# Two-layer trunk: the feed-forward's first tiles kept in PSUM, the last x tile taken last, and 128-column matmuls behind 512-column ones

## The chip, the core and the metric

The kernel runs on one core of a Trainium2 chip. The metric is the device time of one execution in microseconds; the time before is the median of three runs. Engines are named as in the profile: PE (TensorE, matrix multiplies), PEld (its loads of weights), DVE (VectorE), ACT (ScalarE), POOL (GpSimd) and SP (SyncE, which issues most transfers). PSUM, where PE writes its sums, has eight banks of 128 x 512 float32: four in a pool "acc", four in a pool "aux".

## What is computed

A trunk of two layers over 512 positions of width 1024. Each layer is a mixer (gated linear attention and sparse attention in the first, retention in the second) and a feed-forward; the change touches the feed-forward alone, which runs twice, with D_FF = 2816, or 22 tiles of 128.

```python
def rmsnorm(x, g):
    return x * rsqrt(mean(x * x, axis=-1) + EPS) * g

def swiglu(h, w_gate, w_up, w_down):
    return (silu(h @ w_gate) * (h @ w_up)) @ w_down

for layer in range(2):
    h = h + mixer(rmsnorm(h, attn_norm[layer]), ...)
    h = h + swiglu(rmsnorm(h, ffn_norm[layer]), w_gate[layer], w_up[layer], w_down[layer])
return rmsnorm(h, final_norm)
```

## The kernel before

x is held transposed: eight tiles X[0] to X[7] of 128 features x 512 positions. Every float32 product is done in three matmuls of a rounded type. A matrix is split in a high part (ACT rounds it: wh for weights, xh for x) and what is left (DVE subtracts: wl, xl), and `mm3` issues high x high, low x high and high x low. A weight slab is 128 x 1024; `slab()` hands out the next one of a fixed list and prepares two ahead of it: a transfer by SP, wh by ACT and wl by DVE (L176, L178). Three wh and three wl buffers go round, so the wh of a slab waits until PE has done with the slab three before it or one that came free sooner.

`ffn` (L722 and after) has these stages:

- The first two f tiles, f=0 and f=1, by plain projections: gate and up, each 24 matmuls of 512 columns (8 tiles of x, three matmuls each; `proj_b`), 96 in all. The norm's factor rb is applied behind the matmul: g = gate x rb, u = up x rb (L806, L807), then `act`: silu on ACT, the product on DVE, and the split of the result into ah and al.
- Between the projections, `mixed(k)` for k = 0 to 3 makes sums and differences of the halves (in positions and in features) of x: tn, split into ch and cl, and td, split into dh and dl. DVE and ACT take turns at it.
- The other 20 f tiles in ten rounds i = 0 to 9 of seven products, P1, P2, P7, P6, P5, P3 and Q4: a scheme that makes a 2 x 2 block product in seven block products where the plain way takes eight. Each product is 24 matmuls of 256 columns. P7 and P6 read ch and cl, Q4 reads dh and dl, P1, P5, P2 and P3 read halves of xh and xl; `n1()` makes the half that P5 and the later P1 need. P1, P6, P5 and P3 of a round add up in one PSUM bank, q["z"]; behind P1, P6 and P5 ACT copies the running sum out (c, L830 and L838) before the next product adds to it. P7 and Q4 add up in another bank, P2 has a bank of its own.
- From round 2 on, down-projections "D" of tiles that are done stand between the products: 18 matmuls of 512 columns each, into aux, added to X. The list EVENTS sets the order of products and D; `after` makes for each product a generator with its work on DVE and ACT, and `follow()` takes one step of each at every event.

Each engine runs its own instructions in a fixed order, which a scheduler sets when the kernel is built, by its estimates of when things will be ready; at run time an instruction that waits holds up all behind it on its engine. So the order of the code is a wish: the order of instructions on an engine is shown below where the text needs it.

Of the kernel before, what the change touches and what calls it, by code (L numbers as in the profile page):

```python
# [16 lines left out]
P = 128  # L17
# [30 lines left out]
def trunk(ctx: ExitStack, tc: tile.TileContext, a, out):  # L48
# [17 lines left out]
    def tt_(name, dt=F32, n=512):  # L66
        return tp.tile([P, n], dt, tag="t", name=name)
# [117 lines left out]
    def slab():  # L185
        while len(ready) <= AHEAD and state["i"] < len(sched):
            prepare()
        return ready.pop(0)

    def mm3(ps, ops, start=True, stop=True, skip=False):  # L190
        n = len(ops)
        for i, (lh, ll, rh, rl) in enumerate(ops):
            nc.tensor.matmul(ps, lh, rh, start=start and i == 0, stop=False, skip_group_check=skip)  # L193
            nc.tensor.matmul(ps, lh, rl, start=False, stop=False, skip_group_check=skip)  # L194
            nc.tensor.matmul(ps, ll, rh, start=False, stop=stop and i == n - 1, skip_group_check=skip)  # L195

# [90 lines left out]
    def new_rb():  # L287
        return cp.tile([P, T], F32, tag="rb", name="rb")
# [8 lines left out]
    def proj_b():  # L297
        wh, wl = slab()
        ps = acc()
        mm3(ps, [(wh[:, k * P:(k + 1) * P], wl[:, k * P:(k + 1) * P], XH[k], XL[k]) for k in range(KT)])  # L300
        return ps
# [418 lines left out]
    def ffn(box, g0, final, halves=False):  # L720
# [10 lines left out]
        def gain(k):  # L731
            return sm[:, g0 + k:g0 + k + 1]

        def mixed(k):

            x12, tn, td = tt_("x12"), tt_("tn"), tt_("td")
            nc.scalar.activation(x12[:, lo], X[k][:, hi], AF.Copy, scale=gain(k))
            nc.vector.scalar_tensor_tensor(tn[:, lo], X[k + 4][:, hi], gain(k + 4), x12[:, lo],
                                           op0=ALU.mult, op1=ALU.subtract)
            nc.scalar.activation(CH_[k][:, lo], tn[:, lo], AF.Copy)  # L740
            nc.vector.scalar_tensor_tensor(tn[:, hi], X[k][:, lo], gain(k), tn[:, lo], op0=ALU.mult, op1=ALU.add)
            nc.scalar.activation(CH_[k][:, hi], tn[:, hi], AF.Copy, scale=-1.0)
            nc.vector.scalar_tensor_tensor(td[:, lo], X[k + 4][:, lo], gain(k + 4), tn[:, hi],
                                           op0=ALU.mult, op1=ALU.subtract)
            d = HALF[k % 2]
            nc.scalar.activation(DH_[k // 2][:, d], td[:, lo], AF.Copy, scale=-1.0)
            nc.vector.tensor_sub(CL_[k][:, lo], tn[:, lo], CH_[k][:, lo].bitcast(F32))
            nc.vector.scalar_tensor_tensor(CL_[k][:, hi], tn[:, hi], -1.0, CH_[k][:, hi].bitcast(F32),
                                           op0=ALU.mult, op1=ALU.subtract)
            nc.vector.scalar_tensor_tensor(DL_[k // 2][:, d], td[:, lo], -1.0, DH_[k // 2][:, d].bitcast(F32),  # L750
                                           op0=ALU.mult, op1=ALU.subtract)

# [19 lines left out]
            "Q4": [(DH_[k // 2][:, HALF[k % 2]], DL_[k // 2][:, HALF[k % 2]]) for k in range(4)],  # L772
        }

        def product(ps, w, name, start):

            for gu in range(2):
                cols = [slice(gu * 512 + k * P, gu * 512 + (k + 1) * P) for k in range(4)]
                mm3(ps[:, HALF[gu]], [(w[0][:, cols[k]], w[1][:, cols[k]]) + forms[name][k] for k in range(4)],
                    start=start and gu == 0, skip=True)  # L780

        def act(f, g, u, neg):

# [11 lines left out]
            AH[f] = (ah, al)  # L795


        rb = None
        for f in range(2):
            pg = proj_b()  # L800
            if rb is None:
                rb = norm_b(box["acc"], D, new_rb())
            mixed(2 * f)
            pu = proj_b()
            g, u = tt_("g"), tt_("u")
            nc.vector.tensor_mul(g, pg, rb)  # L806
            nc.vector.tensor_mul(u, pu, rb)  # L807
            for _ in act(f, g, u, False):
                pass
            mixed(2 * f + 1)  # L810


        Q = [{} for _ in range(NQ)]
        pend = []

        def rbh(c):
            return rb[:, None, c].to_broadcast([P, 2, H])
# [39 lines left out]
        def add(n, ps):  # L857
            nc.vector.tensor_add(X[n], X[n], ps)  # L858
            yield
# [6 lines left out]
        for e in EVENTS:  # L866
            w = slab()
            follow()
            if e[0] == "D":
                ps = aux()  # L870
                down(e[2], w, ALL, e[1], ps)
                pend.append(add(e[2], ps))
                continue
            name, i = e
            q = Q[i]
            if name == "P1":
                q["z"] = acc()
            elif name == "P7":
                q["v"] = acc()
            elif name == "P2":  # L880
                q["y"] = aux()
            bank = {"P1": "z", "P6": "z", "P5": "z", "P3": "z", "P7": "v", "Q4": "v", "P2": "y"}[name]
            product(q[bank], w, name, name in ("P1", "P7", "P2"))
            pend.append(after(name, i))
            if e == ("P1", 0):
                n1()
        while pend:
            follow()

# [255 lines left out]
```

## Time and profile before

| | us |
|---|---|
| median of 3 runs | 1336.08 (1335.88 to 1336.95) |
| the profiled execution, its own time | 1339.95 |
| its span in the trace | 1338.2 |
| PE busy | 1313.5 (98%) |
| DVE busy | 986.5 (74%) |
| ACT busy | 638.2 (48%) |

The profile is of one execution. In the text, times in a stage are us from the span's start. The first layer's feed-forward starts at 237.07 with its projections and at 259.36 with its products; the second layer's at 977.09 and 999.52. Matmuls are pipelined: the recorded busy time of one overlaps the next, so the cost of one in a row of many is the distance between two starts. Names in the trace have their numbers left out, so acc is any bank of that pool.

### The profile page before, as it was taken

How to read it: one execution, taken by the hardware profiler on the slowest of the kernel's cores; microseconds unless marked ns; L12 is line 12 of the kernel's file. 1: busy time of each engine (PE TensorE's matmuls, PEld its weight loads, DVE VectorE, ACT ScalarE, POOL GpSimd, SP SyncE). 2: the span in 40 equal slices, each digit the busy share in tenths (PEclk: the TensorE clock that was granted, in tenths of full speed). 3: DMA queues.
4: the chain of work that ended last, by engine and by line, in shares of the span. 5: the costliest groups of instructions: out<-in, count | busy, mean ns of one | idle time of the engine just before them, and what ended most of it. 6: DMA issues, size and time to landing. Idle time of an engine off the chain costs nothing.

```text
span 1338.2 us, 18846 instructions
## 1 busy us (share of the span) xinstructions
PE 1313.5 (98%) x7578; PEld 1157.6 (87%) x7578; DVE 986.5 (74%) x1385; ACT 638.2 (48%) x891; POOL 88.3 (7%) x78
## 2 busy tenths in 40 slices
PE   8999999999999999999999999999998999999997
PEld 6788777899999999888888888888888999999986
DVE  6799887998787787675564563663699977878755
ACT  7763575754344353453523523423565534434433
POOL 2231110000000000011120110110000000000002
PEclk9999999999999999999999999999998999999999
DMA  6484322233333232243222232232232333333222
GB/s 227 106 182 110 93 75 66 95 114 119 98 115 99 88 113 68 73 158 100 79 95 87 79 95 89 69 96 93 61 113 91 99 103 109 113 101 110 69 59 79
DMA packets 43336, 133.58 MB, mean 100 GB/s; under 512 B 4832, under 2 KB 8304, under 8 KB 43248
## 3 DMA queue, kind: packets, MB, share of 16 engines
q1 hardware_dynamic: 40144, 123.99, 29.7%
q0 software_dynamic: 2016, 7.34, 3.2%
q8 instruction: 59, 0.97, 0.3%
q10 hardware_dynamic: 1088, 1.05, 0.2%
q14 instruction: 29, 0.24, 0.1%
HBM read 130.26 MB, written 2.10 MB: 99 GB/s over the span
## 4 chain that ended last, share of the span: by engine, by line
PE 88%; DVE 7%; ACT 3%; issue 1%; DMA 1%; DVEq 0%; ACTq 0%
PE acc L193 21%; PE acc L195 21%; PE acc L194 21%; PE aux L194 8%; PE aux L193 8%; PE aux L195 8%; DVE sc L442 1%; DVE m L441 1%; DVE S L558 1%; DMA wl<-in_we 1%; ACT wh L176 1%; DVE wl L178 0%; DVE fin L1026 0%; DVE sc L433 0%; PE aux L658 0%
## 5 line engine op out<-in xcount | busy, mean ns | idle before, releaser
L176 ACT ACTIVATE wh<-w 128x1024 fp32r<-128x1024 f32 (+2 forms) x205 | 200.3, 977 | 340.3 <-PE acc L194 163.3
L193 PE MATMUL acc<-xh,wh 128*128 128x512 f32 (+1 forms) x952 | 321.3, 338 | 5.9 <-ACT wh L350 5.1
L195 PE MATMUL acc<-xh,wl 128*128 128x512 f32 (+1 forms) x952 | 319.9, 336 | 0.0
L194 PE MATMUL acc<-xl,wh 128*128 128x512 f32 (+1 forms) x952 | 319.8, 336 | 0.0
L178 DVE TENSOR_TENSOR wl<-w,wh 128x1024 fp32r<-128x1024 f32 (+2 forms) x191 | 218.2, 1142 | 67.1 <-ACT wh L176 65.9
L193 PEld LDWEIGHTS acc<-xh,wh 128*128 128x128 f32 x952 | 179.5, 189 | 25.0 <-ACT wh L350 5.1
L194 PEld LDWEIGHTS acc<-xl,wh 128*128 128x128 f32 x952 | 181.4, 191 | 19.5 <-DVE xl L236 0.4
L195 PEld LDWEIGHTS acc<-xh,wl 128*128 128x128 f32 x952 | 179.4, 188 | 18.7
L176 ACT ACTIVATE wh<-q 128x1024 fp32r<-128x1024 f32 x100 | 106.4, 1064 | 153.5 <-PE acc L194 62.9
L178 DVE TENSOR_TENSOR wl<-q,wh 128x1024 fp32r<-128x1024 f32 x100 | 122.2, 1224 | 30.0 <-ACT wh L176 29.7
L193 PE MATMUL aux<-ah,wh 128*128 128x512 f32 x288 | 112.6, 391 | 0.0
L194 PE MATMUL aux<-al,wh 128*128 128x512 f32 x288 | 112.6, 391 | 0.0
L195 PE MATMUL aux<-ah,wl 128*128 128x512 f32 x288 | 112.0, 389 | 0.0
L195 PE MATMUL acc<-ch,wl 128*128 128x256 f32 x320 | 91.2, 285 | 4.2 <-DVE wl L178 4.2
L193 PE MATMUL acc<-ch,wh 128*128 128x256 f32 x320 | 91.0, 284 | 0.3 <-ACT c L830 0.3
L194 PE MATMUL acc<-cl,wh 128*128 128x256 f32 x320 | 90.8, 284 | 0.0
L195 PEld LDWEIGHTS acc<-ch,wl 128*128 128x128 f32 x320 | 61.2, 191 | 4.6 <-DVE wl L178 4.6
L193 PE MATMUL acc<-yh,wh 128*128 128x512 f32 x160 | 62.8, 394 | 1.7 <-ACT yh L198 1.5
L858 DVE TENSOR_TENSOR x<-x,aux 128x512 f32<-128x512 f32 x48 | 32.9, 685 | 42.3 <-PE aux L195 42.3
L195 PEld LDWEIGHTS aux<-ah,wl 128*128 128x128 f32 x288 | 54.1, 188 | 11.6
L193 PEld LDWEIGHTS aux<-ah,wh 128*128 128x128 f32 x288 | 54.1, 188 | 10.0
L194 PEld LDWEIGHTS acc<-cl,wh 128*128 128x128 f32 x320 | 62.3, 195 | 0.4
(287 smaller groups left out, 2659.1 us busy)
## 6 DMA issues: line engine op xcount, KB each, us to landing
q<-in_wq SPq DMA_DIRECT2D x60, 512.0 KB, 3.6
w<-in_wo SPq DMA_DIRECT2D x48, 512.0 KB, 3.5
w<-in_wd SPq DMA_DIRECT2D x48, 384.0 KB, 3.1
w<-in_we SPq DMA_DIRECT2D x21, 512.0 KB, 4.4
w<-in_wq SPq DMA_DIRECT2D x20, 512.0 KB, 3.5
w<-in_woo SPq DMA_DIRECT2D x16, 512.0 KB, 3.5
wl<-in_we POOLq DMA_DIRECT2D x14, 512.0 KB, 7.6
w<-in_weo SPq DMA_DIRECT2D x8, 512.0 KB, 3.5
```

What stands on the lines that cost most here:

```text
L176: nc.scalar.activation(wh[:, :n], w[:, :n], AF.Copy)
L178: nc.vector.tensor_sub(wl[:, :n], w[:, :n], wh[:, :n].bitcast(F32))
L193: nc.tensor.matmul(ps, lh, rh, start=start and i == 0, stop=False, skip_group_check=skip)
L194: nc.tensor.matmul(ps, lh, rl, start=False, stop=False, skip_group_check=skip)
L195: nc.tensor.matmul(ps, ll, rh, start=False, stop=stop and i == n - 1, skip_group_check=skip)
L441: nc.vector.max(m, sc)
L442: nc.vector.match_replace(sc, m, sc, MARK)
L558: nc.vector.scalar_tensor_tensor(S[s, c + 1, p, :], S[s, c, p, :], DEC[p][s, c:c + 1], kv, op0=ALU.mult, op1=ALU.add)
L858: nc.vector.tensor_add(X[n], X[n], ps)
```

## The change

In the start of the feed-forward:

- The gate and up sums of f=0 stay in two acc banks, those of f=1 in two aux banks, and all four are multiplied by rb later. In each f, gate and up first take the features' tiles k = 0 to 6 and then both k = 7.
- `mixed` loses its td part, and its tn is kept in tiles of the tag "a". The td, dh and dl part is `mixed4`, called for all four k behind P6(0).
- The norm (`norm_b`) is called behind P2(0); `empty(0)`, which is the multiplication of f=0 by rb and its `act`, is put in the queue of `follow()` there, `empty(1)` behind P7(0), together with `n1()`, which stood behind P1(0).

In the products: `mm3` gets an argument `cut`. With it, the first matmul of 256 columns is issued as two of 128 columns with the same weights. It is set for the first product of the list and for each product that directly follows a D: 23 in each layer, 46 in all.

```diff
+    def mm3(ps, ops, start=True, stop=True, skip=False, cut=False):
         for i, (lh, ll, rh, rl) in enumerate(ops):
+            if cut and i == 0:
+                for j, c in enumerate((slice(0, P), slice(P, 2 * P))):
+                    nc.tensor.matmul(ps[:, c], lh, rh[:, c], start=start and j == 0, stop=False, skip_group_check=skip)
+            else:
+                nc.tensor.matmul(ps, lh, rh, start=start and i == 0, stop=False, skip_group_check=skip)
...
         def mixed(k):
-            x12, tn, td = tt_("x12"), tt_("tn"), tt_("td")
+            x12, tn = tt_("x12"), fp.tile([P, T], F32, tag="a", name="tn", bufs=20)
...
+            TN.append(tn)
+
+        def mixed4(k):
+            td, d = tt_("td"), HALF[k % 2]
+            nc.vector.scalar_tensor_tensor(td[:, lo], X[k + 4][:, lo], gain(k + 4), TN[k][:, hi],
+                                           op0=ALU.mult, op1=ALU.subtract)
+            nc.scalar.activation(DH_[k // 2][:, d], td[:, lo], AF.Copy, scale=-1.0)
             nc.vector.scalar_tensor_tensor(DL_[k // 2][:, d], td[:, lo], -1.0, DH_[k // 2][:, d].bitcast(F32),
                                            op0=ALU.mult, op1=ALU.subtract)
...
-        rb = None
+        G0 = []
         for f in range(2):
-            pg = proj_b()
-            if rb is None:
-                rb = norm_b(box["acc"], D, new_rb())
+            pair_ = [(acc if f == 0 else aux)() for _ in range(2)]
+            ws = [slab(), slab()]
+            for ks in (range(KT - 1), range(KT - 1, KT)):
+                for ps, w in zip(pair_, ws):
+                    mm3(ps, [(w[0][:, k * P:(k + 1) * P], w[1][:, k * P:(k + 1) * P], XH[k], XL[k]) for k in ks],
+                        start=ks[0] == 0, stop=ks[0] > 0)
+            G0.append(pair_)
             mixed(2 * f)
-            pu = proj_b()
+            mixed(2 * f + 1)
+        rb = new_rb()
+
+        def empty(f):
+            pg, pu = G0[f]
             g, u = tt_("g"), tt_("u")
             nc.vector.tensor_mul(g, pg, rb)
             nc.vector.tensor_mul(u, pu, rb)
-            for _ in act(f, g, u, False):
-                pass
-            mixed(2 * f + 1)
+            yield from act(f, g, u, False)
+            yield
...
             if e[0] == "D":
...
+                wide = True
                 continue
...
-            product(q[bank], w, name, name in ("P1", "P7", "P2"))
+            product(q[bank], w, name, name in ("P1", "P7", "P2"), wide)
+            wide = False
+            if e == ("P2", 0):
+                norm_b(box["acc"], D, rb)
+                pend.append(empty(0))
             pend.append(after(name, i))
-            if e == ("P1", 0):
+            if e == ("P7", 0):
                 n1()
+                pend.append(empty(1))
+            elif e == ("P6", 0):
+                for k in range(4):
+                    mixed4(k)
```

How instructions stand then, in the second layer's feed-forward, by three places. A row has the line, the operation, out<-in with the tiles' numbers, the shape and, in brackets, the engines or transfers whose semaphores it waits for.

First ACT, near the copy that takes P6(0)'s running sum out of its bank (c_9091<-acc_8950 before, c_9114<-acc_8924 after), ahead of P5(0). Before:

```order
L746 ACTIVATE dh_8725<-td_8931 128x256 [waits DVE_49]
L759 ACTIVATE xh_8574<-n1_8975,sm_83 128x256 [waits DVE_49]
...
L759 ACTIVATE xh_8605<-n1_8984,sm_83 128x256 [waits DVE_49]
L830 ACTIVATE c_8997<-acc_8950 128x512 [waits Activation_49]
L176 ACTIVATE wh_9058<-w_8886 128x1024 [waits PE_49]
L176 ACTIVATE wh_9087<-q_9056 128x1024 [waits DMAHW5_49,DVE_49,PE_49]
L830 ACTIVATE c_9091<-acc_8950 128x512 [waits PE_49,Activation_49]
```

Now:

```order
L176 ACTIVATE wh_9141<-q_8835 128x1024 [waits PE_49,Activation_49]
L800 ACTIVATE ah_9056<-u_9001 128x512 [waits DVE_49]
L176 ACTIVATE wh_9176<-q_8916 128x1024 [waits DMAHW3_49,PE_49,Activation_49]
L795 ACTIVATE g_9059<-g_9059 128x512 [waits DVE_49]
L760 ACTIVATE dh_8747<-td_9088 128x256 [waits DVE_49]
...
L760 ACTIVATE dh_8748<-td_9100 128x256 [waits DVE_49]
L850 ACTIVATE c_9114<-acc_8924 128x512 [waits Activation_49]
L850 ACTIVATE c_9146<-acc_9116 128x512 [waits DVE_49]
L800 ACTIVATE ah_9111<-u_9060 128x512 [waits DVE_49]
L176 ACTIVATE wh_9213<-w_9174 128x1024 [waits PE_49]
```

The copy stood behind the n1 parts of xh and two slabs' wh; the last dh was six rows and more ahead of it, in front of n1. Now the four dh stand directly ahead of the copy, behind two wh and the silu of f=1 (g_9059); wh_9213 is the slab of P7(1).

Then DVE, from the wl of P7(0) on before (wl_8947; wl_9059 is that of P5(0), wl_9088 that of P2(1)):

```order
L178 TENSOR_TENSOR wl_8947<-w_8888,wh_8946 128x1024
L758 TENSOR_TENSOR n1_8975<-x0_84 128x256
...
L762 SCALAR_TENSOR_TENSOR xl_8606<-n1_8984,sm_83,xh_8605 128x256 [waits Activation_49]
L178 TENSOR_TENSOR wl_8994<-q_8786,wh_8993 128x1024 [waits PE_49]
L178 TENSOR_TENSOR wl_9025<-q_8991,wh_9024 128x1024 [waits PE_49]
L834 TENSOR_TENSOR gu_9028<-c_8997,aux_8999 128x2x256 [waits Activation_49]
L178 TENSOR_TENSOR wl_9059<-w_8886,wh_9058 128x1024 [waits PE_49,Activation_49]
L835 TENSOR_TENSOR gu_9028<-gu_9028,rb_8759 128x2x256 [waits DVE_49]
L124 TENSOR_TENSOR q_8842<-q_8842,q_8786 128x1024
L178 TENSOR_TENSOR wl_9088<-q_9056,wh_9087 128x1024 [waits DMAHW5_49,PE_49,Activation_49]
```

Now, from the wl of P5(0) on (wl_9052; wl_9106 is that of P2(1)); the rows left out first are the rest of f=0's and P2(0)'s multiplications and of n1:

```order
L178 TENSOR_TENSOR wl_9052<-w_8841,wh_9051 128x1024 [waits PE_49,Activation_49]
L258 SCALAR_TENSOR_TENSOR c_8990<-c_8990,y_8991 128x512 [waits DVE_49]
L122 TENSOR_TENSOR q_8950<-w_9172,q_8950 128x1024
L259 SCALAR_TENSOR_TENSOR rb_8915<-c_8990,y_8991 128x512 [waits DVE_49]
L178 TENSOR_TENSOR wl_9106<-q_9049,wh_9105 128x1024 [waits DMAHW5_49,PE_49,Activation_49]
L826 TENSOR_TENSOR g_9000<-acc_8751,rb_8915 128x512 [waits DVE_49]
...
L773 SCALAR_TENSOR_TENSOR xl_8629<-n1_9042,sm_83,xh_8628 128x256 [waits Activation_49]
L797 TENSOR_TENSOR u_9001<-u_9001,g_9000 128x512
L826 TENSOR_TENSOR g_9059<-aux_8833,rb_8915 128x512
L827 TENSOR_TENSOR u_9060<-aux_8834,rb_8915 128x512
L758 SCALAR_TENSOR_TENSOR td_9088<-x4_88,sm_83,tn_8816 128x256 [waits DVE_49]
...
L758 SCALAR_TENSOR_TENSOR td_9100<-x7_91,sm_83,tn_8907 128x256 [waits DVE_49]
```

The steps of rb, g and u of both f tiles and the four td stood in the projections' time before; now they are behind the wl of P5(0). On PE, P5(0) is the row `L198 MATMUL acc_8924<-xh_8597,wh_9051 128x256 [waits Activation_49]`, and P2(1) stands ahead of it, where it stood behind P5(0) before.

Last PE, where the projections end and P1(0) starts. Before:

```order
L194 MATMUL acc_8894<-xl_8702,wh_8789 128x512
L195 MATMUL acc_8894<-xh_8701,wl_8790 128x512
L193 MATMUL acc_8950<-xh_8574,wh_8844 128x256 [waits DVE_49,Activation_49]
L194 MATMUL acc_8950<-xl_8575,wh_8844 128x256
L195 MATMUL acc_8950<-xh_8574,wl_8845 128x256
L193 MATMUL acc_8950<-xh_8583,wh_8844 128x256
```

Now:

```order
L199 MATMUL aux_8834<-xl_8725,wh_8762 128x512
L200 MATMUL aux_8834<-xh_8724,wl_8763 128x512
L196 MATMUL acc_8924<-xh_8597,wh_8837 128x128 [waits Activation_49]
L196 MATMUL acc_8924<-xh_8597,wh_8837 128x128
L199 MATMUL acc_8924<-xl_8598,wh_8837 128x256
L200 MATMUL acc_8924<-xh_8597,wl_8838 128x256 [waits DVE_49]
L198 MATMUL acc_8924<-xh_8606,wh_8837 128x256
```

The first matmul of the product has become two rows of 128 columns with the same wh, and the last step (k = 7) of a projection is ahead of it as before. The 22 products that follow a D begin in the same way.

## Rows read from the trace of the kernel before

**Rows 1.** The page, parts 1 and 2: busy time of each engine with its share of the span and its instructions, and the granted TensorE clock in 40 slices.

```profile
PE 1313.5 (98%) x7578; PEld 1157.6 (87%) x7578; DVE 986.5 (74%) x1385; ACT 638.2 (48%) x891; POOL 88.3 (7%) x78
...
PEclk9999999999999999999999999999998999999999
```

**Rows 2.** Windows, by stage: projections of the first layer's feed-forward, its run of 480 product matmuls (20 products of 24), the same two of the second layer, and 48 matmuls of two later products. Columns: window, length in us, then busy time (instructions) of PE, PEld, DVE, ACT and POOL, mean granted clock, DMA share, GB/s. An instruction that reaches into a window is counted in it.

```profile
237.07:259.36 22.29, 22.29 (x100) 18.40 (x98) 21.83 (x37) 16.13 (x26) 0.00 (x0) 1.00 0.39 142
259.36:317.77 58.41, 57.06 (x481) 56.65 (x480) 56.15 (x72) 34.08 (x47) 0.00 (x0) 1.00 0.33 102
977.09:999.52 22.43, 22.43 (x99) 18.28 (x98) 21.48 (x33) 14.24 (x22) 0.00 (x0) 1.00 0.38 141
999.52:1062.73 63.21, 59.23 (x481) 58.81 (x480) 59.79 (x81) 35.58 (x53) 0.00 (x0) 0.95 0.31 94
...
335.75:341.40 5.65, 5.65 (x50) 5.65 (x48) 4.43 (x6) 2.55 (x3) 0.00 (x0) 1.00 0.39 143
```

**Rows 3.** Waits of TensorE over the whole span: engine and line, what it waited for, us in total, times, longest.

```profile
PE acc L195 <- DVE wl L178: 4.2, 2, 3.2
...
PE acc L193 <- ACT wh L176: 0.8, 1, 0.8
...
PE acc L193 <- ACT c L830: 0.3, 1, 0.3
```

**Rows 4.** Timeline of TensorE in the second layer, near the ends of its waits: start in us, busy us, instruction, and in brackets the idle time ahead of it and what ended it.

```profile
1006.37 0.39 PE L193 MATMUL acc<-xh,wh 128*128 128x256 f32 x1 [0.79 <-ACT wh L176]
...
1010.07 0.58 PE L195 MATMUL acc<-ch,wl 128*128 128x256 f32 x1 [3.18 <-DVE wl L178]
```

**Rows 5.** Windows of the stretch behind those waits, columns as in group 2.

```profile
1008.10:1011.50 3.40, 1.43 (x6) 1.43 (x7) 3.40 (x9) 1.11 (x3) 0.00 (x0) 0.50 0.20 33
1011.50:1014.90 3.40, 3.40 (x18) 3.40 (x17) 3.40 (x6) 1.08 (x3) 0.00 (x0) 0.50 0.31 122
1014.90:1018.00 3.10, 3.10 (x29) 3.10 (x28) 2.86 (x5) 1.24 (x2) 0.00 (x0) 1.00 0.00 0
```

**Rows 6.** Timeline of VectorE in the same place: start and busy time. Instructions overlap at their ends, so the cost of one is the distance to the next start.

```profile
1003.13 0.48 DVE L743 SCALAR_TENSOR_TENSOR td<-x,sm,tn 128x256 f32<-128x256 f32 x1
1003.53 0.69 DVE L806 TENSOR_TENSOR g<-acc,rb 128x512 f32<-128x512 f32 x1
1004.13 0.42 DVE L748 SCALAR_TENSOR_TENSOR cl<-tn,ch 128x256 fp32r<-128x256 f32 x1
...
1008.78 1.23 DVE L178 TENSOR_TENSOR wl<-w,wh 128x1024 fp32r<-128x1024 f32 x1
1009.92 1.44 DVE L758 TENSOR_TENSOR n<-x 128x256 f32<-128x256 f32 x4
1011.26 1.68 DVE L762 SCALAR_TENSOR_TENSOR xl<-n,sm,xh 128x256 fp32r<-128x256 f32 x4
1012.84 2.37 DVE L178 TENSOR_TENSOR wl<-q,wh 128x1024 fp32r<-128x1024 f32 x2
```

**Rows 7.** Timeline of ScalarE in the same place.

```profile
1005.26 1.06 ACT L176 ACTIVATE wh<-q 128x1024 fp32r<-128x1024 f32 x1
...
1007.64 0.42 ACT L746 ACTIVATE dh<-td 128x256 fp32r<-128x256 f32 x1 [0.19 <-DVE td L743]
...
1012.00 0.58 ACT L830 ACTIVATE c<-acc 128x512 f32<-128x512 f32 x1
```

**Rows 8.** Timeline of TensorE in the second layer's mixer, where 128-column matmuls stand ahead of 512-column ones.

```profile
635.17 0.22 PE L193 MATMUL aux<-ath,vh 128*128 128x128 f32 x1
635.22 0.28 PE L194 MATMUL aux<-atl,vh 128*128 128x128 f32 x1
635.34 0.27 PE L195 MATMUL aux<-ath,vl 128*128 128x128 f32 x1
635.45 0.44 PE L193 MATMUL aux<-ath,vh 128*128 128x512 f32 x1
635.73 0.40 PE L194 MATMUL aux<-atl,vh 128*128 128x512 f32 x1
```

**Rows 9.** Lines of TensorE's weight loads: line, operation, shapes and count, busy us and mean ns, idle time before. L193 and L194 of one step hold the same weights.

```profile
L194 PEld LDWEIGHTS acc<-xl,wh 128*128 128x128 f32 x952 | 181.4, 191 | 19.5 <-DVE xl L236 0.4
L193 PEld LDWEIGHTS acc<-xh,wh 128*128 128x128 f32 x952 | 179.5, 189 | 25.0 <-ACT wh L350 5.1 <-ACT wh L176 1.0
```

**Rows 10.** Windows of three runs of 256-column matmuls: 192 of eight products behind 512-column work; 406 of the second layer's run, behind the stretch of group 5; and 35 starts (34 distances) in the last down-projections. Columns as in group 2.

```profile
387.37:409.98 22.61, 22.61 (x193) 22.61 (x192) 17.84 (x20) 12.04 (x15) 0.00 (x0) 1.00 0.36 112
1014.91:1062.73 47.82, 47.82 (x408) 47.82 (x407) 44.40 (x50) 26.06 (x33) 0.00 (x0) 1.00 0.37 114
...
1316.31:1320.39 4.08, 4.08 (x36) 4.08 (x35) 2.13 (x4) 2.02 (x4) 1.45 (x2) 1.00 0.00 0
```

**Rows 11.** Timeline of TensorE where the last down-projections go from 512 to 256 columns.

```profile
1315.97 0.39 PE L195 MATMUL acc<-ah,wl 128*128 128x512 f32 x1
1316.20 0.28 PE L193 MATMUL acc<-ah,wh 128*128 128x256 f32 x1
1316.31 0.28 PE L194 MATMUL acc<-al,wh 128*128 128x256 f32 x1
```

More of the change, by code (lines that the diff above doesn't have):

```diff
@@ L188, in slab @@
         return ready.pop(0)
-    def mm3(ps, ops, start=True, stop=True, skip=False):
+    def mm3(ps, ops, start=True, stop=True, skip=False, cut=False):
         n = len(ops)
         for i, (lh, ll, rh, rl) in enumerate(ops):
-            nc.tensor.matmul(ps, lh, rh, start=start and i == 0, stop=False, skip_group_check=skip)
+            if cut and i == 0:
[3 more added lines that the diff above has]
+                nc.tensor.matmul(ps, lh, rh, start=start and i == 0, stop=False, skip_group_check=skip)
             nc.tensor.matmul(ps, lh, rl, start=False, stop=False, skip_group_check=skip)
@@ L732, in gain @@
             return sm[:, g0 + k:g0 + k + 1]
+        TN = []
         def mixed(k):
-            x12, tn, td = tt_("x12"), tt_("tn"), tt_("td")
+            x12, tn = tt_("x12"), fp.tile([P, T], F32, tag="a", name="tn", bufs=20)
             nc.scalar.activation(x12[:, lo], X[k][:, hi], AF.Copy, scale=gain(k))
@@ L742, in mixed @@
             nc.scalar.activation(CH_[k][:, hi], tn[:, hi], AF.Copy, scale=-1.0)
[L743 to L746, printed above, removed]
             nc.vector.tensor_sub(CL_[k][:, lo], tn[:, lo], CH_[k][:, lo].bitcast(F32))
@@ L773, in ffn, with product @@
         }
-        def product(ps, w, name, start):
+        def product(ps, w, name, start, cut):
             for gu in range(2):
@@ L779, in product @@
                 mm3(ps[:, HALF[gu]], [(w[0][:, cols[k]], w[1][:, cols[k]]) + forms[name][k] for k in range(4)],
-                    start=start and gu == 0, skip=True)
+                    start=start and gu == 0, skip=True, cut=cut and gu == 0)
         def act(f, g, u, neg):
@@ L872, in ffn @@
                 pend.append(add(e[2], ps))
+                wide = True
                 continue
```

## The prediction

> **What bounds the kernel now.** First the busy shares and the granted clock on the page: TensorE (PE) is busy 98% of the span, VectorE (DVE) 74%, ScalarE (ACT) 48% [rows 1]. So a gain has to shorten TensorE's own stream, or close gaps in it. Then the stages, by windows [rows 2]: in each layer the feed-forward opens with 96 projection matmuls of 512 columns, then come 20 products, a run of 480 matmuls of 256 columns. In the undisturbed window 48 such matmuls take 5.65 us, 0.1178 us each, so 480 should take 56.5 us. They take 58.41 us in the first layer and 63.21 us in the second: 1.9 and 6.7 us over, 8.6 in all. The projections lose nothing of note: 22.29 and 22.43 us, 0.1 us apart. With that, **8.8 us** is the most that the change can win at the two starts.
>
> What the loss is made of stands in the waits [rows 3] and the order of time [rows 4]: in the second layer TensorE stands 0.79 us for a rounded weight slab (wh) and 3.18 us for its rest (wl), both behind the work that makes the mixed blocks. Then the granted clock reads 0.50 from 1008.10 to 1014.90 [rows 5], the lower of its two levels (1.2 GHz), after an engine that had stood nearly still, and back at 1.00 the matmuls run as before. Of the 6.7 us 4.0 are standing, and 2.7 the slow clock.
>
> **Part 1, the start.** T is the start of P1(0). The change takes the mixed blocks (ch, cl) before T and lets the gate and up tiles of f=0 and f=1 wait in PSUM. What was done before T is now behind it: the norm (rb), the four multiplications by rb, two gated tiles, the four td tiles and dh, dl. I price DVE's chain from its starts in [rows 6], one to the next: 0.40 us for a 256-column td, 0.60 for 512 columns, 1.14 for a slab's wl, 1.34 for four n1, 1.58 for four xl. ACT's are 1.06 for wh, 0.42 for dh, 0.58 for a copy c [rows 7].
>
> Each product takes 24 x 0.1178 = 2.83 us. P1, P2, the two norm matmuls (0.45) and P7(0) end at T + 9.04 (a cut, below, has 0.1 of it). The slab of P5(0) takes over P7(0)'s buffer: a matmul's tail of 0.17, wh 1.06 and a hand-over of 0.1 put DVE's wl of P5(0) at T + 10.4. Behind it in DVE's order stand one step of rb (0.60), a weight sum (1.14), the last step of rb (0.60), the wl of P2(1) (1.14), g, u and gu (1.80), n1 (1.34), xl (1.58), u (0.60), g and u of f=1 (1.20) and the four td (1.60). With its own 1.14 this is 12.7 us, to T + 23.1. Behind the td ACT does the last dh (0.42 and a hand-over) and only then c<-acc_8924, the copy that takes P6(0)'s sum out of its bank: done at about T + 24.2. P5(0) adds onto that bank, so it **cannot start before T + 24.2**.
>
> Without a wait TensorE would be there at T + 17.5: six products at 2.83, the norm and the cut. So 6.7 us are lost: about 2.9 ahead of P2(1), whose wl is ready at T + 15.1 where its third matmul is reached at T + 12.1, and the rest, 3.8, ahead of P5(0). P7(1) comes next; its slab takes P5(0)'s buffer, and its wh stands behind that on ACT: about 1.4 more (wh 1.06, what is left of a copy 0.25, a hand-over 0.1). Sum **8.1 us per layer**, both layers alike, since the queues are. What is queued behind ACT's wait for the td is this copy above all, and TensorE waits for it; the moved DMAs of SP only trade places among w and q tiles that are needed later, and POOL has nothing here, so I cost both at nothing; the cover is the lead of two slabs (2 x 2.83 us), and without it the wait for a transfer would show in full.
>
> Then the clock. Stands of 3 to 4 us in a row are what came ahead of the 0.50 stretch in the second layer [rows 4, 5], while the 1.9 us of the first layer came without one: its stage reads 1.00 [rows 2]. I take the second layer's 2.7 us for each layer; bounds 0 (the first layer) and 5.4 (two such stretches, one for each stand). The start then costs 2 x (8.1 + 2.7) = 21.6 where it cost 8.8: **+12.8 us**. Bounds of the stall itself: 4 us per layer, if ACT's or DVE's order gives a step for each engine that I have in a row, and 10, if hand-overs between them cost as much as the longest here.
>
> **Part 2, the cut.** 46 products that follow 512-column work (23 in each layer) take their first matmul as two of 128 columns with the same weights. No 256-column row is followed by such a pair; the nearest are three of 128 ahead of 512 [rows 8]. They start 0.05, 0.12 and 0.11 us apart, and the 512-column one behind takes 0.28 where 0.227 is usual: the first is given back later. So one of 128 costs about 0.112 us; two in place of one of 0.118 add 0.105 us, times 46 = **+4.8 us**. Below, both go at the first's 0.058, which adds nothing. That half the columns aren't half the time agrees with the weight loads: each matmul has one of its own, also where L193 and L194 hold the same wh [rows 9]. The Trainium skill ("TensorE: Matmul & The Clock Gate", section "LDWEIGHTS (loading the stationary operand)") puts a load at its columns over 1.2, 107 ns for 128 columns, which speaks against a cut that loads the same weights twice; the 0.112 us of the row agrees. Its section "Back-to-back issue gap" gives some 81 ns for a sustained pair of load and matmul at 128 columns; by that the cut would cost 46 x (2 x 81 - 118) = 2.0 us, an estimate, and the sum would be 1350.9; the row's 0.112 decides here.
>
> What could the cut give back? Only the pace of the run behind it. That pace isn't one constant: products go at 0.1178 [rows 2], the run at 1316 us at 4.08 / 34 = 0.120 [rows 10], and its first interval is 0.114 [rows 11]. But products keep 0.1178 whatever stood ahead: 22.61 us for 192 of them behind 512-column work, 47.82 us for 406 behind the slow stretch [rows 10]. So I forecast no change of pace. Bounds for 3,314 matmuls (2 x 70 x 24 less 46): at 0.114, -12.6 us; at 0.120, +7.3 us.
>
> **Sum.** +12.8 + 4.8 = **+17.6 us**. The profiled execution's own time is 1339.95 us (span 1338.2), 3.9 above the median of the runs shown, so it would become 1357.6, and the median 1336.08 + 17.6 = **1353.7 us**.
>
> **Rivals.**
> 1. The change does at the start what it says, and nothing is late behind it: the 8.8 us go and only the cut is paid. 1336.1 - 8.8 + 4.8 = 1332.1 us. For it: DVE is idle a quarter of the time [rows 1], and the mixed blocks do leave the way of P7(0). Against it: in the stretch from T + 10 to T + 23 DVE's list has no hole, and P6's copy has moved behind it. It decides whether ACT reaches that copy before T + 17.5; it would then be faster.
> 2. The cut changes the pace of the run behind it, and pays for all. At 0.114 it is 1353.7 - 12.6 = 1341.1; at the 0.112 of the 128-column rows, 1334.5, and with a smaller stall below that. For it: three paces for the same form in this trace. Against it: the products' one pace behind two quite different openings [rows 10]. The other way, 0.120, is 1361.0.
> 3. Half of the stall: DVE takes the two gated tiles with fewer hand-overs and the clock holds. 1336.1 - 8.8 + 2 x 4 + 4.8 = 1340.1 us.
>
> **How the numbers follow.** A measurement of this kernel tells about 0.2% (2.7 us) from no change: faster is under 1333.4, slower over 1338.75. Forecast, with its bounds 1345 to 1360: 0.53, all slower. Rival 1: 0.12 (0.09 faster, 0.03 same). Rival 2, quicker pace: 0.22 (0.08 faster, 0.05 same, 0.09 slower); slower pace 0.05, slower. Rival 3: 0.08 (0.02 same, 0.06 slower). Together 0.17 faster, 0.10 same, 0.73 slower. The range 1332 to 1361 leaves out the half of rival 1 that wins more, the far end of rival 2 and the slower pace: about 0.14. The forecast alone has 1345 to 1360.
>
> **What would show it.** In the profile after: the run of 480 in each layer takes 56.5 + 8 to 11 us (65 to 67), with TensorE waiting for ACT c ahead of P5(0) some 3.8 us, for DVE wl ahead of P2(1) some 2.9, and a granted clock of 0.50 for some 5 us behind. The copy of P6 stands on ACT behind four dh. Behind each D the cut's two rows take 0.22 us or so together, and all later rows 0.1178. I am wrong if P5(0) starts within a microsecond of T + 17.5 (rival 1), if the steady 256-column pace is anything but 0.1178 (rival 2), or if 128-column rows behind 512-column ones take 0.06.

## The result

The changed kernel takes 1347.45 us, the median of 4 runs (1346.98 to 1348.19), where the kernel before takes 1336.08, the median of 3 (1335.88 to 1336.95): a ratio of 1.0084, 95% interval 1.0064 to 1.0104. A fourth execution of the kernel before took 3388.7 us and counts in neither figure. The changed kernel is **slower by 11 us**; the forecast was 17.6 us, 1353.7 in a range from 1332 to 1361. The profiled execution took 1348.19 us (span 1346.3), 8.2 us more than that of the kernel before.

The stages of the kernel after, by windows: the first layer's projections and run of 480, the second layer's, and the first layer's part from the first D to the last. Columns: length in us, busy time (instructions) of PE, PEld, DVE, ACT and POOL, granted clock, DMA share, GB/s.

```profile
236.96:258.72 21.76, 21.76 (x97) 18.02 (x96) 17.02 (x28) 10.38 (x20) 0.00 (x0) 1.00 0.40 146
258.72:327.39 68.67, 61.56 (x485) 60.20 (x483) 62.39 (x80) 39.16 (x54) 0.00 (x0) 0.95 0.28 87
984.30:1006.06 21.76, 21.76 (x97) 18.02 (x96) 19.14 (x32) 10.73 (x20) 0.00 (x0) 1.00 0.38 145
1006.06:1073.31 67.25, 60.18 (x484) 58.63 (x483) 61.46 (x80) 39.19 (x54) 0.00 (x0) 0.95 0.29 89
327.39:564.63 237.24, 237.24 (x1656) 219.92 (x1654) 181.54 (x203) 101.76 (x127) 0.00 (x0) 1.00 0.31 95
```

Against [rows 2] the projections are 0.5 and 0.7 us shorter, above all because the two norm matmuls (0.45 us) have left them. The runs of 480 take 68.67 and 67.25 us where they took 58.41 and 63.21, 14.3 us more in all. And the part from the first D to the last takes 237.24 us, where the kernel before has

```profile
317.77:557.41 239.64, 239.64 (x1633) 222.37 (x1632) 182.68 (x203) 101.76 (x127) 0.00 (x0) 1.00 0.31 94
```

The second layer has the same two lengths. So each layer wins 2.40 us in a part that only the cut touches; it is called the D part below. The sum is 14.3 - 1.2 - 4.8 = 8.3 us, where the profiled executions differ by 8.2. The medians differ by 3 us more, because the profiled execution of the kernel before took 3.9 us more than its median and that of the kernel after 0.7 more; where those 3.9 us lie isn't shown, since only one execution of it has a trace.

The waits of TensorE in the kernel after, over the span (engine, line, what it waited for, us in total, times, longest):

```profile
PE acc L198 <- ACT c L850: 6.6, 2, 3.3
...
PE aux L200 <- DVE wl L178: 3.4, 2, 1.7
PE acc L198 <- ACT wh L176: 2.1, 2, 1.0
PE aux L198 <- ACT wh L176: 2.1, 2, 1.0
```

Each stands twice, once in a layer. In the second layer's order of time (start, busy time, instruction, idle time ahead of it and what ended it):

```profile
1019.21 0.39 PE L198 MATMUL aux<-xh,wh 128*128 128x256 f32 x1 [1.03 <-ACT wh L176]
...
1021.41 0.39 PE L200 MATMUL aux<-xh,wl 128*128 128x256 f32 x1 [1.70 <-DVE wl L178]
...
1031.93 0.38 PE L198 MATMUL acc<-xh,wh 128*128 128x256 f32 x1 [3.30 <-ACT c L850]
...
1037.58 0.39 PE L198 MATMUL acc<-ch,wh 128*128 128x256 f32 x1 [1.03 <-ACT wh L176]
```

The first two are P2(1), for its wh and then its wl; 1031.93 is P5(0), for the copy; the last is P7(1). Together 7.0 us per layer. With T at 1006.06 the P5(0) row starts at T + 25.9. Why so late is seen on DVE and ACT in the same stretch. DVE:

```profile
1020.14 1.22 DVE L178 TENSOR_TENSOR wl<-q,wh 128x1024 fp32r<-128x1024 f32 x1
...
1024.42 1.66 DVE L773 SCALAR_TENSOR_TENSOR xl<-n,sm,xh 128x256 fp32r<-128x256 f32 x4
...
1027.80 1.66 DVE L758 SCALAR_TENSOR_TENSOR td<-x,sm,tn 128x256 f32<-128x256 f32 x4
```

From 1020.14 (the wl of P2(1)) to the end of the four td at 1029.46 nothing is idle: the chain that the prediction added up, which ends at T + 23.4 for a forecast of T + 23.1. ACT:

```profile
1028.60 1.06 ACT L176 ACTIVATE wh<-q 128x1024 fp32r<-128x1024 f32 x1 [0.29 <-ACT ah L800]
1029.56 0.61 ACT L795 ACTIVATE g<-g 128x512 f32<-128x512 f32 x1
1030.08 1.32 ACT L760 ACTIVATE dh<-td 128x256 fp32r<-128x256 f32 x4
1031.30 1.06 ACT L850 ACTIVATE c<-acc 128x512 f32<-128x512 f32 x2
```

The wh of Q4's slab starts at 1028.60, when P2(1), whose last matmul starts at 1028.35, has given its buffer back; then come the silu of f=1, the four dh, and only then two copies; the first is P6(0)'s.

The granted clock behind these stands, by windows:

```profile
1022.70:1026.00 3.30, 3.30 (x19) 3.30 (x19) 3.30 (x9) 1.71 (x4) 0.00 (x0) 0.55 0.00 0
1026.00:1028.40 2.40, 2.40 (x23) 2.40 (x21) 2.40 (x6) 1.58 (x2) 0.00 (x0) 1.00 0.00 0
1028.40:1031.90 3.50, 0.23 (x2) 0.02 (x1) 2.45 (x8) 3.30 (x8) 0.00 (x0) 1.00 0.01 2
1031.90:1035.30 3.40, 3.37 (x18) 3.37 (x19) 3.40 (x6) 1.09 (x2) 0.00 (x0) 0.59 0.01 1
```

It reads 0.55 in the 3.3 us behind the two stands at P2(1) and 0.59 in the 3.4 us behind the one at P5(0), the lower level for most of each stretch, and 1.00 between.

And the cut, at a D in the first layer, with the two 128-column matmuls in one row (x2):

```profile
338.23 0.39 PE L200 MATMUL aux<-ah,wl 128*128 128x512 f32 x1
338.45 0.34 PE L196 MATMUL acc<-xh,wh 128*128 128x128 f32 x2
338.63 0.33 PE L199 MATMUL acc<-xl,wh 128*128 128x256 f32 x1
338.79 0.28 PE L200 MATMUL acc<-xh,wl 128*128 128x256 f32 x1
338.91 0.28 PE L198 MATMUL acc<-xh,wh 128*128 128x256 f32 x1
```

then the pace of a long run behind a cut, 186 distances from the sixth matmul on:

```profile
397.35:418.43 21.08, 21.08 (x189) 21.08 (x187) 16.52 (x20) 11.21 (x15) 0.00 (x0) 1.00 0.39 119
```

The two matmuls of 128 columns and the 256-column one behind them start at 338.45, 338.51 and 338.63, and the next at 338.79: 0.34 us go where two of 256 columns took 0.236 before, so a cut costs 0.10 us. But from the sixth matmul on the pace is 21.08 / 186 = 0.1133 us, where [rows 10] have 0.1178.

### The profile page after: what moved, and what is told of

Read it like the earlier page. It is cut to its first block, busy times and chain, and to the rows that moved or that the text cites. A ratio compares the mean times of both kernels' runs of the same rounds, so it can differ in the third digit from the quotient of the medians.

```text
span 1346.3 us, 18931 instructions
## 1 busy us (share of the span) xinstructions
PE 1313.4 (98%) x7624; PEld 1155.5 (86%) x7624; DVE 985.8 (73%) x1385; ACT 636.8 (47%) x891; POOL 88.1 (7%) x78
## 4 chain that ended last, share of the span: by engine, by line
PE 92%; DVE 4%; ACT 2%; issue 1%; DMA 1%; SPq 0%; DVEq 0%; ACTq 0%
PE acc L199 22%; PE acc L200 21%; PE acc L198 21%; PE aux L199 8%; PE aux L200 8%; PE aux L198 8%; DVE wl L178 1%; ACT wh L176 1%; DMA q<-in_wq 1%; PE acc L196 1%; DVE sc L447 1%; PE aux L555 0%; DVE m L446 0%; PE aux L434 0%; DVE fin L1055 0%
## 5 line engine op out<-in xcount | busy, mean ns | idle before, releaser
L198 PE MATMUL acc<-xh,wh 128*128 128x512 f32 (+1 forms) x896 | 303.8, 339 | 11.7 <-ACT c L850 6.6
L199 PE MATMUL acc<-xl,wh 128*128 128x256 f32 (+1 forms) x920 | 309.6, 336 | 0.1
L200 PE MATMUL acc<-xh,wl 128*128 128x256 f32 (+1 forms) x920 | 308.6, 335 | 0.4 <-DVE wl L178 0.4
L198 PEld LDWEIGHTS acc<-xh,wh 128*128 128x128 f32 x896 | 172.0, 192 | 29.7 <-ACT c L850 7.0
L199 PEld LDWEIGHTS acc<-xl,wh 128*128 128x128 f32 x920 | 176.6, 192 | 17.9 <-DVE xl L241 1.1
L200 PEld LDWEIGHTS acc<-xh,wl 128*128 128x128 f32 x920 | 176.3, 192 | 18.1 <-DVE wl L178 0.8
L198 PE MATMUL aux<-ah,wh 128*128 128x512 f32 x288 | 112.6, 391 | 0.0
L198 PE MATMUL acc<-ch,wh 128*128 128x256 f32 x310 | 86.2, 278 | 2.1 <-ACT wh L176 2.1
L198 PE MATMUL acc<-yh,wh 128*128 128x512 f32 x160 | 62.8, 395 | 1.7 <-ACT yh L203 1.5
L198 PEld LDWEIGHTS aux<-ah,wh 128*128 128x128 f32 x288 | 54.1, 188 | 10.0
L199 PE MATMUL acc<-yl,wh 128*128 128x512 f32 x160 | 62.6, 391 | 0.0
L200 PE MATMUL acc<-yh,wl 128*128 128x512 f32 x160 | 62.5, 390 | 0.0
```

## Experiments

Two theories on the start: the **order** (rb is late, and the copy stands behind the dh), or the **amount** (DVE has more to do between P1(0) and P5(0) than TensorE leaves it time for). Two on the cut: a mere cost, or a quicker pace. "Standing" below is worked out from the distances between matmul starts in a run of 480: of each over 0.29 us what is over 0.118; for the slow clock the same of those from 0.14 to 0.29; the norm's two matmuls are left out. By that the kernel before has 1.7 and 4.6 us of standing and 0.2 and 2.1 us of slow clock, the kernel after 7.8 and 7.7, and 3.8 and 3.9.

**cut_alone**: the kernel before, with the cut.

```diff
+            if cut and i == 0:
+                for j, c in enumerate((slice(0, P), slice(P, 2 * P))):
+                    nc.tensor.matmul(ps[:, c], lh, rh[:, c], start=start and j == 0, stop=False, skip_group_check=skip)
-            product(q[bank], w, name, name in ("P1", "P7", "P2"))
+            product(q[bank], w, name, name in ("P1", "P7", "P2"), wide)
+            wide = False
```

> The kernel before with the cut alone: its start untouched, the first matmul of each product behind 512-column work as two of 128 columns. Theory (the cut sets a quicker pace for the whole run behind it, 0.1135 us a matmul where it was 0.1178, and costs some 0.105 us each): the part from the first D to the last loses 2.4 us per layer as in the changed kernel, and the 480 matmuls at the start up to 2.0 us per layer more, so 1327 to 1332 us. Rival (the cut is only a cost and the quicker pace has come from the changed order): 46 x 0.105 = +4.8, 1341 us.

Measured 1333.5 us, ratio 0.9967 (0.9957 to 0.9976). The two runs of 480 and the D part of the first layer, by windows:

```profile
260.56:318.98 58.42, 57.06 (x483) 56.56 (x482) 56.30 (x72) 34.12 (x47) 0.00 (x0) 1.00 0.32 102
...
998.30:1060.56 62.26, 58.35 (x482) 57.35 (x481) 59.06 (x80) 35.90 (x52) 0.00 (x0) 0.97 0.30 96
318.98:556.22 237.24, 237.24 (x1656) 219.94 (x1654) 181.72 (x203) 101.74 (x127) 0.00 (x0) 1.00 0.31 95
```

The D part is 237.24 us to the hundredth as in the kernel after: the gain is the cut's. The time is 1.5 us over the expected 1327 to 1332, because the runs of 480 win nothing in the first layer and 1 us in the second: the mean of their undisturbed distances is 0.1172 and 0.1153, so part of the quicker pace is lost there. In the first layer the distances are 0.1133 up to a stand of 1.2 us at 270.01 and 0.1178 from there to the end.

**start_alone**: the changed kernel without the cut.

```diff
-            product(q[bank], w, name, name in ("P1", "P7", "P2"), wide)
+            product(q[bank], w, name, name in ("P1", "P7", "P2"), False)
```

> The changed kernel without the cut. Theory (start and cut add up): waits at the start as in the changed kernel, 7.0 us per layer, every product at 0.1178 us a matmul, and the time some 14 to 16 us above the kernel before, 1350 to 1353 us. Rival (the cut only costs): 1347.5 - 4.8 = 1342.7 us.

Measured 1352.38 us, ratio 1.0109 (1.0092 to 1.0125), inside the expected 1350 to 1353.

```profile
259.17:327.57 68.40, 61.12 (x483) 59.88 (x482) 62.31 (x80) 39.17 (x54) 0.00 (x0) 0.95 0.28 87
...
1008.64:1076.12 67.48, 60.14 (x484) 58.68 (x482) 61.63 (x80) 39.21 (x54) 0.00 (x0) 0.95 0.29 88
327.57:567.21 239.64, 239.64 (x1633) 222.37 (x1632) 182.26 (x203) 101.59 (x127) 0.00 (x0) 1.00 0.31 94
```

The D part is that of the kernel before. Projections and runs together take 179.4 us (two times 21.76, 68.40 and 67.48) where [rows 2] have 166.3: the start costs **13.1 us** more in this profile. One expectation failed: not every product goes at 0.1178. Behind the norm's two matmuls, which are held up by 0.2 us together, with no cut anywhere, 45 distances of the first layer are 5.10 us:

```profile
265.67:270.77 5.10, 5.10 (x47) 5.10 (x46) 4.04 (x5) 3.34 (x4) 0.00 (x0) 1.00 0.30 97
```

That is 0.1133 again. And the long end of each run of 480, behind the same stand at P7(1) in both layers, goes at another pace in each. These are 240 distances of the first layer and the same 240 of the second:

```profile
293.30:321.57 28.27, 28.27 (x243) 28.27 (x242) 27.19 (x31) 16.57 (x21) 0.00 (x0) 1.00 0.37 114
1043.14:1070.34 27.20, 27.20 (x243) 27.20 (x241) 26.68 (x31) 16.55 (x21) 0.00 (x0) 1.00 0.39 119
```

28.27 / 240 = 0.1178 and 27.20 / 240 = 0.1133. The quicker pace is not a property of the cut; a wait can end in it too, and no run shows what decides. So the 13.1 us are not the stall alone: the quick distances take some 1.9 us off it (a mean of 0.1142 in the second layer's run and 0.1170 in the first's).

**td_behind_p5**: the changed kernel, td, dh and dl called behind P5(0).

```diff
-            elif e == ("P6", 0):
+            elif e == ("P5", 0):
                 for k in range(4):
                     mixed4(k)
```

> The changed kernel with the td, dh and dl part called behind P5(0), so that ACT has the copy of P6(0)'s sum ahead of the four dh. Theory (P5(0) waits for that copy, the copy for the dh ahead of it, and these for four td at the end of DVE's list): the copy now waits for the silu of f=1 only, some 2 us earlier, so TensorE's wait for it falls from 3.3 to about 1.2 us per layer and the time to about 1343 us, a little less if the clock holds. Rival (something else readies P5(0) at the same moment, the xl of n1 or its slab): the wait gets another name, the time stays at 1347 us.

Measured 1348.32 us, ratio 1.0083 (1.0068 to 1.0098): no gain. The waits in the second layer:

```profile
PE acc L198 <- ACT c L850: 2.1, 1, 2.1
PE aux L200 <- DVE wl L178: 1.9, 1, 1.9
...
PE acc L198 <- ACT c L858: 0.6, 1, 0.6
```

The wait for P6(0)'s copy falls from 3.3 to 2.1, not to 1.2, and 0.6 comes back ahead of P3(0), which waits for P5(0)'s copy; that one now stands behind the dh. Standing is 7.6 and 7.9 us per layer as before, the slow clock 3.7 and 4.9. What the expectation left out is ACT's order: the wh of Q4's slab, which starts at 1027.08 when P2(1) ends, and the silu still stand ahead of the copy. The dh did hold the copy back, but taking this one piece out did not make the start shorter.

**less_ahead_of_p5**: the same, with f=1's multiplications and gated tile behind Q4(0).

```diff
             if e == ("P7", 0):
                 n1()
+            elif e == ("Q4", 0):
                 pend.append(empty(1))
```

> As td_behind_p5, with the multiplications and the gated tile of f=1 behind Q4(0) as well. Theory (the stand ahead of P5(0) is the DVE work that stands in front of the copy of P6(0)'s sum, and what is left of it is f=1's 1.2 us of multiplications and its silu): P5(0) waits for less than 0.5 us, P2(1) still for 1.0 + 1.7 us because rb is as late as before; waits of 3 to 5 us per layer, 1338 to 1342 us. Rival (DVE as a whole is late by 7 us, and whatever is taken away only brings the next piece to the end of the chain): waits of 7 us, 1347 us.

Measured 1341.85 us, ratio 1.0033 (1.0020 to 1.0045), the time as expected.

```profile
PE aux L200 <- DVE wl L178: 1.7, 1, 1.7
PE acc L198 <- ACT wh L176: 1.4, 1, 1.4
PE acc L198 <- ACT c L858: 1.2, 1, 1.2
PE aux L198 <- ACT wh L176: 1.0, 1, 1.0
```

P5(0) no longer waits for the copy, and 5.3 us remain, a little over the 3 to 5 expected: 2.7 at P2(1) as forecast, and 2.6 further on, at P7(1) and P3(0), which were not. By distances the standing is 6.6 and 5.9 us.

**norm_early**: the changed kernel with the norm ahead of P1(0), and f=0 and f=1 queued behind P1(0) and P2(0).

```diff
         rb = new_rb()
+        norm_b(box["acc"], D, rb)
...
-            if e == ("P2", 0):
-                norm_b(box["acc"], D, rb)
-                pend.append(empty(0))
+            if e in (("P1", 0), ("P2", 0)):
+                pend.append(empty(0 if e[0] == "P1" else 1))
...
-                pend.append(empty(1))
```

> The changed kernel with the norm ahead of P1(0) and both f tiles' multiplications queued behind P1(0) and P2(0), n1 behind P7(0), td behind P6(0) as before. Theory (what binds the start is how much DVE has to do between P1(0) and P5(0), some 5 us of which the change took out of the projections' time, where DVE now stands idle): rb comes 5 us earlier, but all the same work still stands ahead of P5(0)'s wl and P2(1)'s wl, so waits of 5 to 7 us per layer stay, where 7.7 were, under other names; 1342 to 1347 us. Rival (the late rb is the cause, the order alone): waits of at most 3 us per layer, no slow clock, 1333 us or less.

Measured 1341.02 us, ratio 1.0021 (1.0009 to 1.0033), 1 us under the expected 1342 to 1347.

```profile
PE acc L198 <- ACT c L851: 5.3, 1, 5.3
```

All waits of the start have become one, of 5.3 us, ahead of P5(0), for the same copy. The late rb alone is not the cause: with rb early the work still ends late. But it is a part: 7.7 us of standing became 5.7, and one long stand in place of two has only one slow stretch behind it (2.5 and 1.3 us).

**norm_early_less**: norm_early with td behind P5(0) and f=1 behind Q4(0).

```diff
-            if e in (("P1", 0), ("P2", 0)):
+            if e in (("P1", 0), ("Q4", 0)):
                 pend.append(empty(0 if e[0] == "P1" else 1))
...
-            elif e == ("P6", 0):
+            elif e == ("P5", 0):
```

> As norm_early, with the td part behind P5(0) and f=1 behind Q4(0): both causes at once. Theory (late rb makes the stand ahead of P2(1), the work ahead of the copy the one ahead of P5(0); the cut adds its quicker pace): waits of at most 1.5 us per layer, no slow clock, the run of 480 in 55 to 57 us in both layers, and some 1325 to 1328 us, as cut_td_n1 or a little better. Rival (P3(0) or Q4(0) then waits for the td or for f=1's place in PSUM): 3 us and more per layer and the slow clock, 1333 us or more.

Measured 1329.99 us, ratio 0.9946 (0.9931 to 0.9961), 2 us over the expected 1325 to 1328.

```profile
PE aux L200 <- DVE wl L178: 1.3, 1, 1.3
PE acc L198 <- ACT c L851: 0.4, 1, 0.4
```

With both changed, the stands fall to 2.3 and 2.9 us (at most 1.5 were expected) and the slow clock to 0.6: by the ratios 10 us less than norm_early, and 11.9 us less than less_ahead_of_p5. That is still 3 us above the best version below. The td and f=1 were moved together; which of the two does more with an early rb isn't shown.

**cut_and_td**: the kernel before, with the cut, and of the change at the start only this: td, dh and dl behind P5(0). Norm, multiplications and gated tiles stay in the projections' time.

```diff
-            nc.vector.scalar_tensor_tensor(td[:, lo], X[k + 4][:, lo], gain(k + 4), tn[:, hi],
-                                           op0=ALU.mult, op1=ALU.subtract)
...
             if e == ("P1", 0):
                 n1()
+            elif e == ("P5", 0):
+                for k in range(4):
+                    mixed4(k)
```

> The kernel before with the cut, and with only the td part moved behind P5(0): norm, multiplications by rb and both gated tiles stay in the projections' time. Theory (the projections' time of DVE was too full by a little, and the td part with its 4 x 0.40 + 4 x 0.34 = 3.0 us is the piece that P7(0) does not need): most of the 0.8 + 3.2 us of waits in the second layer and of the slow clock behind them go, some 4 to 6 us less than with the cut alone, 1323 to 1327 us. Rival (the waits only move, to P5(0) or Q4(0)): the same as the cut alone within 1 us.

Measured 1331.01 us, ratio 0.9953 (0.9938 to 0.9967), 2.5 us under cut_alone where 4 to 6 were expected.

```profile
259.87:316.57 56.70, 56.53 (x482) 56.13 (x481) 55.62 (x75) 34.42 (x50) 0.00 (x0) 1.00 0.32 102
995.91:1056.64 60.73, 58.62 (x483) 57.82 (x481) 59.50 (x84) 35.83 (x53) 0.00 (x0) 0.97 0.31 98
```

The first layer's run of 480 has lost its stands (0.3 us left). In the second layer the stand is shorter, and the clock still falls behind it (0.97):

```profile
PE acc L197 <- ACT ch L746: 1.9, 1, 1.9
```

The theory for the next run is that this ch is late because it stands behind n1 on DVE and ACT.

**cut_td_n1**: the same with n1 behind P2(0).

```diff
-            if e == ("P1", 0):
+            if e == ("P2", 0):
                 n1()
```

> As cut_and_td, with n1 called behind P2(0) and not P1(0), so that the ch of the last mixed block need not stand behind n1 on DVE and ACT. Theory (the 1.9 us wait for ch in the second layer is due to n1 ahead of it): that wait and the slow clock behind it go, 2 to 4 us less than cut_and_td, 1327 to 1329 us. Rival (DVE is full there, and n1 is only late instead, ahead of P1(1)): within 1 us of cut_and_td, 1331 us.

Measured **1326.99 us, ratio 0.9923 (0.9907 to 0.9940)**, the fastest here: some 10 us under the kernel before, 20 under the changed one.

```profile
259.32:315.19 55.87, 55.38 (x483) 54.78 (x481) 54.74 (x74) 35.58 (x50) 0.00 (x0) 1.00 0.35 107
994.54:1051.71 57.17, 56.06 (x483) 55.20 (x481) 56.74 (x82) 35.83 (x53) 0.00 (x0) 1.00 0.31 97
```

The wait for ch falls from 1.9 to 0.4 us. Both runs are at a clock of 1.00; 55.87 us is within 1.5 of 480 x 0.1133.

**cut_td_n1_recut**: cut_td_n1 with P7, P5 and P3 of the first round cut as well.

```diff
-            product(q[bank], w, name, name in ("P1", "P7", "P2"), wide)
+            product(q[bank], w, name, name in ("P1", "P7", "P2"), wide or e in (("P7", 0), ("P5", 0), ("P3", 0)))
```

> As cut_td_n1, with the first matmul of P7, P5 and P3 of the first round cut too. Theory (a wait lets the pace fall back to 0.1178 and a cut behind it sets it to 0.1135 again): the run of 480 has 0.1135 us from the last of these cuts on in both layers, 1.0 to 1.5 us less per layer where cut_td_n1 goes at 0.1178, against 3 x 0.105 of cost; 0.5 to 2 us less in all. Rival (the cut sets the pace only directly behind 512-column work): 0.1178 stays, 0.6 us more.

Measured 1328.76 us, ratio 0.9935 (0.9920 to 0.9950): not the gain that was expected, but cut_td_n1 happened to go at 0.1134 and 0.1140 already, so there was nothing to win. The trace tells what the time can't. Windows of 61 distances behind a hold-up of 0.2 us in the first layer, and of 41 behind the cut that follows, with no 512-column work near:

```profile
266.68:273.86 7.18, 7.18 (x62) 7.18 (x62) 7.18 (x14) 4.31 (x7) 0.00 (x0) 1.00 0.23 72
274.68:279.32 4.64, 4.64 (x43) 4.64 (x42) 4.61 (x8) 3.01 (x6) 0.00 (x0) 1.00 0.10 11
```

7.18 / 61 = 0.1178 ahead of the cut, 4.64 / 41 = 0.1132 behind it. So a cut set the pace in the middle of a run too, at the one place where a run at 0.1178 led up to one.

**cut_no_shift**: cut_alone with the products' slabs at the start of their buffers and not 16 elements in.

```diff
-            wh, wl = parts(16)
+            wh, wl = parts(0)
```

> As cut_alone, with the products' slabs at the start of their buffers and not 16 elements in. Theory (the cut alone sets the pace): the same 0.1135 us a matmul behind each cut, the same time as cut_alone, 1333 us. Rival (the pace is a matter of where the slabs lie, and the cut works on the shifted ones only): 0.120 us as in the last down-projections, which have no shift, so 3,314 x 0.0065 = 21 us more, 1355 us.

Measured 1350.99 us, ratio 1.0100 (1.0080 to 1.0120). First the D part of the first layer, then 186 distances of its long run behind a cut:

```profile
318.77:563.13 244.36, 244.36 (x1656) 227.04 (x1654) 182.57 (x203) 101.50 (x127) 0.00 (x0) 1.00 0.31 92
```

```profile
390.53:412.85 22.32, 22.32 (x189) 22.32 (x187) 17.40 (x21) 11.19 (x15) 0.00 (x0) 1.00 0.37 113
```

22.32 / 186 = 0.1200 with the cut and without the shift, and the D part is 7.1 us longer than with it. That is the pace of the last down-projections, which have neither cut nor shift [rows 10]; on such slabs the cut brings nothing. The theory is out, and the rival's 1355 is 4 us too high, because it took all products of cut_alone to go at 0.1135. The products without either cut or shift were not run.

## Why the prediction was right, and where it was not

- **The start, right.** Forecast +12.8 us; start_alone shows +13.1 in the stages, and 1.0109 in time. Its parts: standing 8.1 us per layer forecast, 7.0 named by the waits and 7.7 with what hangs on them; ahead of P2(1) 2.9 against 2.7, ahead of P5(0) 3.8 against 3.3, ahead of P7(1) 1.4 against 1.0. The runs of 480 take 68.67 and 67.25 us, where 65 to 67 were forecast. The slow clock, 2.7 forecast, is 3.8: there are two slow stretches per layer, one behind each longer stand, and the upper bound of 5.4 counted just that. The close sum is in part luck: standing and slow clock together are 23.2 us in the kernel after where 21.6 were forecast, and in start_alone the quick distances take 1.9 us off again.
- **DVE's chain, right to 0.3 us** (T + 23.4 against T + 23.1). The copy came 1.6 us later than forecast, since the wh of Q4's slab, which waits for P2(1)'s end, stands ahead of the silu and the dh on ACT; TensorE was late at P5(0) by nearly the same, because of the slow stretch ahead of it.
- **Why it is late**, a point on which the prediction named a copy and its queue: the runs show amount and order together. DVE is busy 17.02 and 19.14 us in the projections, where it was 21.83 and 21.48 [rows 2], and 62.39 us in the first run of 480, where it was 56.15. With the td moved alone (td_behind_p5) some 7.7 us of standing were left; with td and f=1 moved (less_ahead_of_p5) 5.9 to 6.6; with rb early and nothing moved (norm_early) 5.7; with both (norm_early_less) 2.3 to 2.9.
- **The cost of a cut, right**: 0.105 us forecast, 0.10 measured.
- **The failed step** is "So I forecast no change of pace", in part 2. The run behind a cut goes at 0.1133, not at 0.1178. In each layer's D part the 22 cuts cost 22 x 0.103 = 2.3 us, and the part is 2.4 shorter all the same, so the pace brings 4.7: net -4.8 in both layers, where +4.8 was forecast. By the prediction's own sign (a steady pace other than 0.1178) part 2 was wrong. This was rival 2, with 0.114 as its pace, +5.0 us as its sum and 1341.1 as its time. The profiled executions differ by 8.2 us: the quick distances bring some 11.4 us and not 12.6, and the stall is 2 us larger than forecast. They bring less than 3,314 matmuls at 0.1133 would, because the pace falls back to 0.1178 at a stand in the first layer's run of 480 (its undisturbed distances have a mean of 0.1174, the second layer's 0.1137), and because the five matmuls behind each cut come ahead of it.
- **Luck in the time.** Between the profiled executions the forecast is 9.4 us too high (17.6 against 8.2), nearly all of it for the pace; between the medians it is 6.2 too high, because the profiled execution before, 1339.95, was 3.9 us above its median and the one after 0.7. So that 1347.5 lies in the forecast's own 1345 to 1360 says nothing for part 2.
- The argument that failed is the one of the two openings: 192 matmuls behind 512-column work and 406 behind a stand, all at 0.1178, do not show that a third opening gives it too. The 0.120 and 0.114 of the last down-projections were in view.
- Rival 1, a start without stands, fell for this change. That it can nearly be had (1.0 and 1.9 us of standing, no slow stretch) is shown by cut_td_n1, which leaves under the projections what DVE can do there and moves only pieces that the first products don't need (td and n1).

That leaves open what in TensorE makes the two steady paces. The runs show what chooses: where the slab lies (0.1200 without the shift, in the last down-projections of every run and in all of cut_no_shift), and, with the shift, how the run begins: in every trace all 44 runs behind a D go at 0.1178 without a cut and at 0.1133 with one; behind a stand either comes, and what decides there is open too.

## What to carry to other kernels

A stage that TensorE seems to fill alone can still be full on another engine: what is moved out from under it has to fit in somewhere else, and here 2 to 5 us of VectorE's work per layer, put behind the start of the products, left TensorE standing 7.7 us, where it had stood 1.7 and 4.6, and losing almost 4 more at the slow clock. Move only the piece that is needed last, and look which slab, copy or PSUM bank comes behind it in each queue. And measure the steady distance of a matmul behind each kind of opening and placement before taking it for a constant: 4% of it were to be had for two narrower matmuls at the head of a run, which by this estimate pays from some 30 matmuls on (0.103 / 0.0045 = 23, and the five at its head).

## What was unexpected of the hardware

256-column matmuls have three steady distances in these kernels, each constant over dozens to hundreds: 0.1133, 0.1178 and 0.1200 us at a granted clock of 1.00. Two matmuls of 128 columns at the head bring the first within five matmuls, also in the middle of a run, and, of the two placements tried, only with slabs 16 elements into their buffers. A stand of TensorE can end in either of the first two: in start_alone the same stand at P7(1) ends in 0.1178 in the first layer and in 0.1133 in the second.
